# First two tiles of the first down-projection side by side, and three first tiles that meet their last inputs late

## The chip, the cores and the metric

The kernel runs on one core of a Trainium2 chip. The metric is device time of one launch in microseconds (us), as the median of three runs; lower is better. Five engines work side by side and meet only through semaphores: TensorE (PE, with its weight loads as PEld), VectorE (DVE), ScalarE (ACT), GpSimd (POOL) and SyncE (SP), whose queue here does nothing but issue the weight DMAs.

## What is computed

A decoder trunk of two layers over 256 positions and 1024 channels. Layer 0 mixes with a gated MLP and an RWKV-7 recurrence, layer 1 with attention; each layer then has a gated feed-forward part with a causal convolution of width 3. Each half of a layer starts from an RMS norm:

```python
def conv_glu_ffn(h, w_up, conv_w, conv_b, w_down):
    z = h @ w_up
    ...
    z = conv_w[0] * z2 + conv_w[1] * z1 + conv_w[2] * z + conv_b
    gate, val = jnp.split(z, 2, axis=-1)
    return (jax.nn.silu(gate) * val) @ w_down

x = x + conv_glu_ffn(rmsnorm(x, ff_norm[layer]), ...)
```

`w_up` is 1024 x 5632, `w_down` is 2816 x 1024.

## The kernel before

Activations stand with channels on the 128 partitions and the 256 positions along the free axis. The residual `R` has eight such tiles (k = 0 to 7), the hidden layer `H` of a feed-forward part has 22. Every matrix product is made at nearly full fp32 precision from three matmuls per 128 x 128 weight block: operands are split into a high and a low part (`xh`, `xl`; `whi`, `wlo`; `hh`, `hl`), and high x high, high x low and low x high are added in PSUM (`mm3`). A block therefore costs three matmuls of 128 x 256.

**Weights** come in pieces of up to 128 x 1024 in the fixed order of the list `plan`. For each piece SP loads `raw`, ACT makes `whi` (L245) and then DVE makes `wlo` (L246). There are four buffers of each, so the split of a piece waits until PE has finished the piece four places earlier. `piece()` hands pieces out in that order and has two further ones made ahead. DVE and ACT each work through one list of instructions that mixes these splits with the epilogues; so does PE with its matmuls.

**PSUM** gives three buffers `pg` to the large products (`gps()`), each with room for two halves of 256 columns, and five `pm` to others.

**A feed-forward part** (`ffn`) has 22 up-tiles. Tile i is two pieces, the gate half and the value half, eight blocks each, 48 matmuls. Its epilogue goes round four engines: DVE `z` (L963, product times the norm's row `rb`), ACT and DVE the convolution (L967 to L969), ACT silu (L970), POOL gate times value (L971), ACT `hh` (L286), DVE `hl`. In DVE's list `z` of tile i+1 stands behind `hl` of tile i. Then come eight down-tiles d in layer 0: three pieces each, over H tiles 0 to 7, 8 to 14 and 15 to 21 (`DN`), 66 matmuls, one after the other. Each ends in `out_tile`: DVE adds the product to `R`, ACT and DVE make that tile's `xh` and `xl` for the next half of a layer, ACT squares it, POOL adds the square to `sqacc`.

**The first tile of such a half** meets the last of these inputs. Its products can start with k = 0 while tile 7 of `R` is still being made. In the middle of it, after ten of its sixteen blocks, PE sums the squares over the partitions (`norm_stats`, PSUM tile `pst`), DVE and POOL make `rs` from it, and after fifteen blocks PE spreads it into a row (`norm_rows`, `prb`), which DVE copies to `rb`. The epilogue's `z` needs `rb`. In layer 1 the first tile is `values(0)`, whose product goes through `gemm_tm` and needs `rs` alone.

The order on an engine is made by a list scheduler when the program is built, except in the mixers, where PE's order is written out.

Of the kernel before, what the change touches and what calls it, by code (L numbers as in the profile page):

```python
# [12 lines left out]
OP = mybir.AluOpType  # L13
# [4 lines left out]
T = 256  # L18
# [141 lines left out]
def body(nc, tc, A, out):  # L160
# [11 lines left out]
    def mm(o, l, r, start=True, stop=True, shared=False):  # L172
        cnt[0] += 1
        PE.matmul(o, l, r, start=start, stop=stop, skip_group_check=shared)  # L174

    def tt(o, a, b, op, eng=None):
        (eng or V).tensor_tensor(o, a, b, op)  # L177
# [23 lines left out]
    V.tensor_scalar(oka, pc[:, _PC["k_a"]:_PC["k_a"] + 4], -1.0, 1.0, op0=OP.mult, op1=OP.add)  # L201

    DN = ((0, 8), (8, 7), (15, 7))
    AHEAD, LAST = 2, 3
    last = {}

# [8 lines left out]
    def plan_ffn(l):  # L215
        for i in range(2 * FT):
            plan.append((A[f"w_up{l}"][i], KT, 128))
        if l == 1:
            plan.extend((A["w_dn1"][i], 2, 512) for i in range(FT))
            return  # L220
        for d in range(KT):
            for k0, kn in DN:
                plan.append((A[f"w_dn{l}"][d][:, 128 * k0:128 * (k0 + kn)], kn, 128))

    plan_ffn(0)
    plan += [(A["w_qkv"][i], 4, 256) for i in range(8)]
# [120 lines left out]
    def gps():  # L347
        return ps.tile([128, 2, T], F32, name="pg", tag="g", bufs=3)
# [4 lines left out]
    def gemm_fm(o, x):  # L353

        for g in range(2):
            w = piece()
            for k in range(KT):
                mm3(o[:, g], w, k, slice(0, 128), x, k, k == 0, k == KT - 1)
                yield 327

    def gemm_tm(o, x):

        ws = [piece(), piece()]
        for b in range(2):
            sl = slice(128 * b, 128 * b + 128)
            for k in range(KT):
                wh, wl = ws[k // 4][0][:, k % 4], ws[k // 4][1][:, k % 4]
                mm(o[:, b], x[0][:, k, sl], wh, k == 0, False)
                mm(o[:, b], x[0][:, k, sl], wl, False, False)
                mm(o[:, b], x[1][:, k, sl], wh, False, k == KT - 1)  # L370
                yield 327

    def run(g):
        for _ in g:
# [570 lines left out]
    def ffn(l, n, nxt, gname):  # L945
        pool = tc.tile_pool(name=f"ff{l}", bufs=1)
        fp = pool.__enter__()
        H = [fp.tile([128, FT, T], F32R, name=f"h{x}{l}") for x in "hl"]
        if l == 1:
            Rt = fp.tile([128, 2, D], F32, name="Rt")  # L950
            last["pool"] = fp
        for i in range(FT):
            o = gps()
            for y_, _ in enumerate(gemm_fm(o, X)):
                if i == 0 and y_ == 9:
                    norm_stats(n)
                if i == 0 and y_ == 14:
                    norm_rows(n)
            z = fp.tile([128, 2, T + 2], F32, name="z", tag="z", bufs=3)
            if i == 0:  # L960
                fp.tile([128, 248], F32, name="pad_z")
            G.memset(z[:, :, 0:2], 0.0)  # L962
            tt(z[:, :, 2:T + 2], o, n["rb2"], OP.mult)  # L963
            y = fp.tile([128, 2, T], F32, name="y", tag="y", bufs=3)
            for g in range(2):
                ch = i + FT * g
                S.activation(y[:, g], z[:, g, 2:T + 2], AF.Identity, scale=P(f"cw{l}2", ch), bias=P(f"cb{l}", ch))  # L967
                V.scalar_tensor_tensor(y[:, g], z[:, g, 1:T + 1], P(f"cw{l}1", ch), y[:, g], op0=OP.mult, op1=OP.add)  # L968
                V.scalar_tensor_tensor(y[:, g], z[:, g, 0:T], P(f"cw{l}0", ch), y[:, g], op0=OP.mult, op1=OP.add)  # L969
            S.activation(y[:, 0], y[:, 0], AF.Silu)  # L970
            tt(y[:, 0], y[:, 0], y[:, 1], OP.mult, G)  # L971
            split(H[0][:, i], H[1][:, i], y[:, 0])
            if l == 1 and i in (2, 3, 4, 5):
                b, e = i % 2, (i - 2) // 2
                pt = mps()
                for d in range(4):
                    PE.transpose(pt[:, 128 * d:128 * d + 128], R[:, 4 * e + d, 128 * b:128 * b + 128], ident)
                S.copy(Rt[:, b, 512 * e:512 * e + 512], pt)
        if l == 1:
            finish(H, fp, Rt)  # L980
            pool.__exit__(None, None, None)
            return
        for d in range(KT):
            o = gps()
            for k0, kn in DN:
                w = piece()
                for k in range(kn):
                    mm3(o[:, 0], w, k, slice(0, 128), H, k0 + k, k0 + k == 0, k0 + k == FT - 1)
            out_tile(nxt, gname, d, o[:, 0])
        pool.__exit__(None, None, None)  # L990


# [57 lines left out]
    def layer_odd(n, nxt):  # L1050
# [14 lines left out]
        od.tile([128, 16], F32, name="pad_q")  # L1065

        def values(c):
            o = gps()
            for y_, _ in enumerate(gemm_tm(o, X)):
                if c == 0 and y_ == 9:  # L1070
                    norm_stats(n)
                if c == 0 and y_ == 14:
                    norm_rows(n)
            for b in range(2):
                S.activation(vt[:, b, 256 * c:256 * c + 256], o[:, b], AF.Copy, scale=n["rs"][:, b:b + 1])

        def project(j):
            o = gps()
# [118 lines left out]
```

## Time and profile before

| | |
|---|---|
| median of three runs | 685.47 us (684.75 to 685.96) |
| the profiled execution, whole | 685.22 us |
| its span, first to last instruction | 683.4 us |
| PE busy in the span | 646.0 us (95%) |
| DVE busy | 509.3 us (75%) |
| ACT busy | 394.7 us (58%) |
| POOL busy | 108.8 us (16%) |
| mean granted TensorE clock | 0.983 of full |

A busy engine here is one with an instruction in flight; overlapping matmuls count once. The last row says that PE's clock was not full in a few stretches: the profile gives the granted clock, 1.00 or 0.50, of any stretch.

In time the kernel runs: layer 0's mixer to about 174 us, its feed-forward's up-tiles to about 302, its down-tiles to about 372, attention to about 486, the second feed-forward to the end.

### The profile page before, as it was taken

To read this page: it belongs to the slowest core of one execution; us is meant where nothing else is said; L and a number is where in the kernel's file an instruction comes from. 1 tells how busy PE (TensorE), PEld (TensorE's weight loads), DVE (VectorE), ACT (ScalarE), POOL (GpSimd) and SP (SyncE) were. 2 spreads that over 40 slices of the span, in tenths; PEclk is the share of its full clock that TensorE was granted. 3 is DMA by queue.
4 is the path that set the end of the run, shared out by engine and by line. 5 is a ranking of instruction groups with operands and counts; after the bars stand their busy time and mean duration, and the time that the engine had idled before them with its cause. 6 is when DMAs were issued, how large, how long until landed. Compare 5 with 4: busy or idle time off the path is not lost.

```text
span 683.4 us, 14445 instructions
## 1 busy us (share of the span) xinstructions
PE 646.0 (95%) x5766; PEld 611.9 (90%) x5766; DVE 509.3 (75%) x944; ACT 394.7 (58%) x710; POOL 108.8 (16%) x154
## 2 busy tenths in 40 slices
PE   7998988799999999997999999999999999999995
PEld 6897767689899999997999999998899999997895
DVE  6899966747888888886666468885888888888543
ACT  6776433323776666665444457775577666666531
POOL 4100000200422222221112000001222222221000
PEclk9999999989999999998999999999999999999999
DMA  7756264104455555556666563332755555555741
GB/s 250 243 166 210 71 174 102 64 1 152 127 186 186 175 169 181 181 156 171 189 194 205 153 213 123 128 124 66 246 183 181 164 182 186 176 167 188 240 125 62
DMA packets 44915, 110.33 MB, mean 161 GB/s; under 512 B 16432, under 2 KB 18096, under 8 KB 44848
## 3 DMA queue, kind: packets, MB, share of 16 engines
q1 hardware_dynamic: 31104, 105.03, 48.4%
q10 hardware_dynamic: 13584, 3.86, 2.4%
q8 instruction: 45, 0.74, 0.4%
q0 software_dynamic: 160, 0.52, 0.3%
q14 instruction: 22, 0.18, 0.1%
HBM read 106.50 MB, written 2.90 MB: 160 GB/s over the span
## 4 chain that ended last, share of the span: by engine, by line
PE 45%; DVE 29%; POOL 10%; ACT 7%; issue 4%; DMA 3%; ACTq 1%; POOLq 0%; DVEq 0%; SPq 0%
PE pg L174 32%; PE pm L174 11%; DVE wlo L246 10%; POOL y L177 8%; DVE y L968 4%; DVE z L177 4%; ACT y L970 2%; ACT hh L286 2%; DVE y L969 2%; DVE WR L177 2%; ACT whi L245 1%; DVE xl L303 1%; DMA scrA<-BK 1%; DVE ftmp L177 1%; PE pm L1117 1%
## 5 line engine op out<-in xcount | busy, mean ns | idle before, releaser
L174 PE MATMUL pg<-xh,whi 128*128 128x256 f32 x1008 | 286.9, 285 | 0.9 <-ACT whi L245 0.4
L174 PE MATMUL pg<-xh,wlo 128*128 128x256 f32 x1008 | 282.5, 280 | 5.1 <-DVE wlo L246 4.8
L174 PE MATMUL pg<-xl,whi 128*128 128x256 f32 x1008 | 281.4, 279 | 1.2 <-DVE xl L303 1.0
L246 DVE TENSOR_TENSOR wlo<-raw,whi 128x1024 fp32r<-128x1024 f32 (+2 forms) x199 | 234.1, 1182 | 51.9 <-ACT whi L245 51.2
L245 ACT ACTIVATE whi<-raw 128x1024 fp32r<-128x1024 f32 (+2 forms) x199 | 201.1, 1018 | 84.9 <-PE pg L174 55.4
L174 PEld LDWEIGHTS pg<-xh,wlo 128*128 128x128 f32 x1008 | 190.7, 189 | 8.4 <-DVE wlo L246 8.4
L174 PEld LDWEIGHTS pg<-xh,whi 128*128 128x128 f32 x1008 | 190.4, 189 | 6.9 <-issue 3.9
L174 PEld LDWEIGHTS pg<-xl,whi 128*128 128x128 f32 x1008 | 190.6, 189 | 2.7 <-DVE xl L303 1.9
L177 POOL TENSOR_TENSOR y<-y 128x256 f32<-128x256 f32 x44 | 63.5, 1444 | 29.3 <-ACT y L970 28.8
L286 ACT ACTIVATE hh<-y 128x256 fp32r<-128x256 f32 x44 | 18.4, 417 | 71.1 <-POOL y L177 71.1
L174 PE MATMUL pg<-hh,whi 128*128 128x256 f32 x176 | 50.4, 287 | 4.7 <-ACT hh L286 4.7
L177 DVE TENSOR_TENSOR hl<-y,hh 128x256 fp32r<-128x256 f32 x44 | 18.7, 425 | 45.3 <-ACT hh L286 45.3
L967 ACT ACTIVATE y<-z,pc 128x256 f32<-128x256 f32 x88 | 48.1, 594 | 5.9 <-DVE z L177 0.7
L174 PE MATMUL pg<-hh,wlo 128*128 128x256 f32 x176 | 50.4, 287 | 0.0
L174 PE MATMUL pg<-hl,whi 128*128 128x256 f32 x176 | 50.4, 287 | 0.0
L177 POOL TENSOR_TENSOR sqacc<-sqacc,sq 128x256 f32<-128x256 f32 x21 | 18.6, 887 | 169.6 <-ACT sq L311 169.1
L174 PEld LDWEIGHTS pg<-hh,whi 128*128 128x128 f32 x176 | 34.6, 196 | 4.9 <-ACT hh L286 4.9
L969 DVE SCALAR_TENSOR_TENSOR y<-z,pc,y 128x256 f32<-128x256 f32 x88 | 38.5, 479 | 0.0
L968 DVE SCALAR_TENSOR_TENSOR y<-z,pc,y 128x256 f32<-128x256 f32 x88 | 38.5, 479 | 0.0
L174 PEld LDWEIGHTS pg<-hh,wlo 128*128 128x128 f32 x176 | 33.9, 193 | 0.2
L174 PEld LDWEIGHTS pg<-hl,whi 128*128 128x128 f32 x176 | 33.9, 192 | 0.2 <-DVE hl L177 0.2
L962 POOL MEMSET z<- 128x4 f32 x44 | 4.2, 102 | 167.9 <-ACT y L970 151.9
(247 smaller groups left out, 1041.3 us busy)
## 6 DMA issues: line engine op xcount, KB each, us to landing
raw<-w_up SPq DMA_DIRECT2D x88, 512.0 KB, 3.5
raw<-w_dn SPq DMA_DIRECT2D x30, 512.0 KB, 3.6
raw<-w_qkv SPq DMA_DIRECT2D x24, 512.0 KB, 3.5
raw<-w_in SPq DMA_DIRECT2D x20, 512.0 KB, 5.2
raw<-w_dn SPq DMA_DIRECT2D x16, 448.0 KB, 3.4
raw<-ev_wo SPq DMA_DIRECT2D x8, 512.0 KB, 4.0
raw<-od_wo SPq DMA_DIRECT2D x8, 512.0 KB, 4.1
R<-xT SPq DMA_DIRECT2D x4, 256.0 KB, 4.0
```

The lines of the kernel that those rows point to most:

```text
L174: PE.matmul(o, l, r, start=start, stop=stop, skip_group_check=shared)
L177: (eng or V).tensor_tensor(o, a, b, op)
L245: S.activation(hi[:, c], raw[:, c], AF.Copy)
L246: last["lo"] = V.tensor_tensor(lo[:, c], raw[:, c], hi[:, c].bitcast(F32), OP.subtract).ins
L286: S.activation(hi, src, AF.Copy)
L303: V.scalar_tensor_tensor(x[1][:, k], R[:, k], P(gname, k), x[0][:, k].bitcast(F32), op0=OP.mult, op1=OP.subtract)
L962: G.memset(z[:, :, 0:2], 0.0)
L967: S.activation(y[:, g], z[:, g, 2:T + 2], AF.Identity, scale=P(f"cw{l}2", ch), bias=P(f"cb{l}", ch))
L968: V.scalar_tensor_tensor(y[:, g], z[:, g, 1:T + 1], P(f"cw{l}1", ch), y[:, g], op0=OP.mult, op1=OP.add)
L969: V.scalar_tensor_tensor(y[:, g], z[:, g, 0:T], P(f"cw{l}0", ch), y[:, g], op0=OP.mult, op1=OP.add)
L970: S.activation(y[:, 0], y[:, 0], AF.Silu)
L1117: PE.transpose(pt[:, 128 * i:128 * i + 128], sc[:, 128 * i:128 * i + 128], ident)
```

## The change

Three edits with one idea, and nothing of the arithmetic changes but the order of additions between tiles.

1. The first two down-tiles of layer 0 are made side by side: `DOWN` lists their pieces in the order (0, first), (1, first), (0, second), (1, second), (0, third), (1, third), and then d = 2 to 7 as before. The loads, splits and products all follow that list, and two `pg` buffers are held at once.
2. `gemm_first`, for the first up-tile of both feed-forward parts: gate and value half get a `pg` buffer each, and the blocks go k = 0 to 4 of the gate half, 0 to 4 of the value half, then 5 to 7 of each. The `z` of this tile becomes two instructions of 256 columns.
3. `gemm_tm` does the same for `values(0)`, with the two blocks of positions in place of the halves.

```diff
+    DOWN = [(d, *part) for part in DN for d in range(2)] + [(d, *part) for d in range(2, KT) for part in DN]
...
+    def gemm_first(o, x):
+
+        ws = [piece(), piece()]
+        for ks in (range(0, 5), range(5, KT)):
+            for g in range(2):
+                for k in ks:
+                    mm3(o[g], ws[g], k, slice(0, 128), x, k, k == 0, k == KT - 1)
+                    yield 327
...
+        late = isinstance(o, list)
+        for ks in ((range(0, 5), range(5, KT)) if late else (range(KT),)):
+            for b in range(2):
+                sl, ob = slice(128 * b, 128 * b + 128), o[b] if late else o[:, b]
+                for k in ks:
...
-            o = gps()
-            for y_, _ in enumerate(gemm_fm(o, X)):
+            o = [gps()[:, 0], gps()[:, 0]] if i == 0 else gps()
+            for y_, _ in enumerate(gemm_first(o, X) if i == 0 else gemm_fm(o, X)):
...
-            tt(z[:, :, 2:T + 2], o, n["rb2"], OP.mult)
+            if i == 0:
+                for g in range(2):
+                    tt(z[:, g, 2:T + 2], o[g], n["rb"], OP.mult)
+            else:
+                tt(z[:, :, 2:T + 2], o, n["rb2"], OP.mult)
...
-        for d in range(KT):
-            o = gps()
-            for k0, kn in DN:
-                w = piece()
-                for k in range(kn):
-                    mm3(o[:, 0], w, k, slice(0, 128), H, k0 + k, k0 + k == 0, k0 + k == FT - 1)
-            out_tile(nxt, gname, d, o[:, 0])
+        os = {}
+        for d, k0, kn in DOWN:
+            if k0 == 0:
+                os[d] = gps()[:, 0]
+            w = piece()
+            for k in range(kn):
+                mm3(os[d], w, k, slice(0, 128), H, k0 + k, k0 + k == 0, k0 + k == FT - 1)
+            if k0 + kn == FT:
+                out_tile(nxt, gname, d, os.pop(d))
```

What it makes of the engines' lists, at three places. First PE, where the first piece of down-tile 0 ends; before (`pg_3924` is down-tile 0, `whi_3881` its second piece):

```order
L174 MATMUL pg_3924<-hh0_2259,whi_3851 128x256
L174 MATMUL pg_3924<-hl0_2260,whi_3851 128x256
L174 MATMUL pg_3924<-hh0_2259,wlo_3852 128x256
L174 MATMUL pg_3924<-hh0_2259,whi_3881 128x256
L174 MATMUL pg_3924<-hl0_2260,whi_3881 128x256
```

and now (`pg_3957` is down-tile 1, `whi_3883` its first piece):

```order
L174 MATMUL pg_3926<-hh0_2259,whi_3853 128x256
L174 MATMUL pg_3926<-hl0_2260,whi_3853 128x256
L174 MATMUL pg_3926<-hh0_2259,wlo_3854 128x256
L174 MATMUL pg_3957<-hh0_2259,whi_3883 128x256
L174 MATMUL pg_3957<-hl0_2260,whi_3883 128x256
```

Where tile 0 went on to its second piece, tile 1 now has its first; on ACT, DVE and SP the pieces are exchanged in the same way, and nothing else of their lists moves there.

Second DVE, at the first up-tile of layer 0's feed-forward; before (`wlo_2352` and `wlo_2382` are the pieces of up-tile 2, which take the buffers of up-tile 0's two pieces; `rs` to `z` is the norm and the tile's `z`):

```order
L246 TENSOR_TENSOR wlo_2264<-raw_2262,whi_2263 128x1024
L303 SCALAR_TENSOR_TENSOR xl_86<-R_73,pc_74,xh_85 128x256 x2
L246 TENSOR_TENSOR wlo_2294<-raw_2292,whi_2293 128x1024
L333 TENSOR_SCALAR rs_2307<-pst_2304 128x1 x2
L246 TENSOR_TENSOR wlo_2352<-raw_2350,whi_2351 128x1024
L343 COPY rb_2329<-prb_2326 128x256
L177 TENSOR_TENSOR z_2334<-pg_2261,rb_2329 128x2x256
L246 TENSOR_TENSOR wlo_2382<-raw_2380,whi_2381 128x1024
L968 SCALAR_TENSOR_TENSOR y_2338<-z_2334,pc_74,y_2338 128x256 x2
```

and now (`wlo_2354` and `wlo_2384` are those of up-tile 2):

```order
L247 TENSOR_TENSOR wlo_2265<-raw_2263,whi_2264 128x1024
L304 SCALAR_TENSOR_TENSOR xl_86<-R_73,pc_74,xh_85 128x256 x2
L334 TENSOR_SCALAR rs_2308<-pst_2305 128x1 x2
L247 TENSOR_TENSOR wlo_2271<-raw_2269,whi_2270 128x1024
L247 TENSOR_TENSOR wlo_2354<-raw_2352,whi_2353 128x1024
L344 COPY rb_2330<-prb_2327 128x256
L247 TENSOR_TENSOR wlo_2384<-raw_2382,whi_2383 128x1024
L177 TENSOR_TENSOR z_2335<-pg_2261,rb_2330 128x256
L177 TENSOR_TENSOR z_2335<-pg_2262,rb_2330 128x256
L984 SCALAR_TENSOR_TENSOR y_2340<-z_2335,pc_74,y_2340 128x256
```

The second split of up-tile 2 stood behind `z` and now stands ahead of it, and `rs` moved ahead of one split. In the second feed-forward that split is moved past `z` too.

Third PE in `values(0)`, ahead of `pst`; before (`whi_4591` and `whi_4618` are the tile's two pieces, k = 0 to 3 and 4 to 7):

```order
L174 MATMUL pg_4670<-whi_4618,xl_86 128x256
L174 MATMUL pg_4670<-whi_4591,xh_85 128x256
L174 MATMUL pg_4670<-wlo_4592,xh_85 128x256
L174 MATMUL pg_4670<-whi_4591,xl_86 128x256
...
L174 MATMUL pst_4713<-cst_79,sqacc_2255 128x1 x2
```

and now:

```order
L174 MATMUL pg_4673<-whi_4620,xh_85 128x256
L174 MATMUL pg_4673<-wlo_4621,xh_85 128x256
L174 MATMUL pg_4673<-whi_4620,xl_86 128x256
L174 MATMUL pst_4716<-cst_79,sqacc_2255 128x1 x2
L174 MATMUL pg_4672<-whi_4620,xh_85 128x256
```

Before, all eight blocks of the first half stood ahead of `pst`, k = 7 among them; now k = 0 to 4 of both halves stand there, and k = 5 to 7 (`pg_4672`) come behind it. `pst` keeps its place after 30 matmuls.

## Rows read from the trace of the kernel before

**Rows 1.** Waits of PE, whole kernel: waiter, awaited, us in total, times, longest.

```profile
PE pg L174 <- ACT hh L286: 4.7, 1, 4.7
PE pg L174 <- DVE xl L303: 1.5, 4, 0.5
...
PE pst L174 <- POOL sqacc L177: 0.8, 1, 0.8
```

**Rows 2.** Stretches at the first down-tile: busy us (count) by engine, granted clock, DMA.

```profile
312.50:315.09 2.59, 0.00 (x0) 0.00 (x0) 1.53 (x4) 0.88 (x3) 1.39 (x1) 0.50 0.67 176
315.09:319.33 4.24, 4.24 (x18) 4.07 (x19) 3.45 (x5) 2.55 (x4) 0.00 (x0) 0.50 0.61 177
```

**Rows 3.** Timeline of PE, down-tiles 0 and 1: start, us, instruction, [idle before].

```profile
305.35 0.28 PE L174 MATMUL pg<-hh,whi 128*128 128x256 f32 x1
...
310.12 0.28 PE L174 MATMUL pg<-hh,wlo 128*128 128x256 f32 x1
315.09 0.58 PE L174 MATMUL pg<-hh,whi 128*128 128x256 f32 x1 [4.70 <-ACT hh L286]
...
319.34 0.29 PE L174 MATMUL pg<-hh,whi 128*128 128x256 f32 x1
...
325.36 0.28 PE L174 MATMUL pg<-hh,whi 128*128 128x256 f32 x1
```

**Rows 4.** Waits of DVE over 20 up-tiles, 196 to 310 us.

```profile
DVE hl L177 <- ACT hh L286: 21.6, 20, 1.1
```

**Rows 5.** Timeline of DVE and ACT, last up-tiles and down-tile 0.

```profile
304.51 1.08 DVE L246 TENSOR_TENSOR wlo<-raw,whi 128x896 fp32r<-128x896 f32 x1
...
310.20 1.23 DVE L246 TENSOR_TENSOR wlo<-raw,whi 128x1024 fp32r<-128x1024 f32 x1
...
312.93 1.08 DVE L246 TENSOR_TENSOR wlo<-raw,whi 128x896 fp32r<-128x896 f32 x1
...
315.91 1.09 DVE L246 TENSOR_TENSOR wlo<-raw,whi 128x896 fp32r<-128x896 f32 x1 [0.41 <-ACT whi L245]
...
314.62 0.42 ACT L286 ACTIVATE hh<-y 128x256 fp32r<-128x256 f32 x1 [1.56 <-POOL y L177]
```

**Rows 6.** Timeline of PE, POOL and ACT, first up-tile of layer 0.

```profile
174.20 0.28 PE L174 MATMUL pg<-xh,whi 128*128 128x256 f32 x1
...
181.19 0.50 PE L174 MATMUL pst<-cst,sqacc 128*128 128x1 f32 x4
...
183.71 0.71 PE L174 MATMUL prb<-cst,rs 128*128 128x128 f32 x4
...
177.87 1.96 POOL L177 TENSOR_TENSOR sqacc<-sqacc,sq 128x256 f32<-128x256 f32 x2 [0.59 <-ACT sq L311]
182.04 1.62 POOL L334 TENSOR_TENSOR rs<-rs,cst 128x2 f32<-128x2 f32 x1 [2.21 <-DVE rs L333]
...
184.70 1.06 ACT L245 ACTIVATE whi<-raw 128x1024 fp32r<-128x1024 f32 x1 [3.06 <-PE pg L174]
...
186.79 1.06 ACT L245 ACTIVATE whi<-raw 128x1024 fp32r<-128x1024 f32 x1
```

**Rows 7.** Timeline of PE, POOL and ACT, first up-tile of layer 1.

```profile
490.87 0.60 PE L174 MATMUL pst<-cst,sqacc 128*128 128x1 f32 x4 [0.79 <-POOL sqacc L177]
...
491.81 0.71 POOL L334 TENSOR_TENSOR rs<-rs,cst 128x2 f32<-128x2 f32 x1 [1.00 <-DVE rs L333]
...
495.01 1.06 ACT L245 ACTIVATE whi<-raw 128x1024 fp32r<-128x1024 f32 x1 [2.22 <-PE pg L174]
...
497.78 1.06 ACT L245 ACTIVATE whi<-raw 128x1024 fp32r<-128x1024 f32 x1 [0.66 <-ACT y L967]
```

**Rows 8.** Timeline of PE, `values(0)`.

```profile
374.59 0.28 PE L174 MATMUL pg<-wlo,xh 128*128 128x256 f32 x1
375.37 0.39 PE L174 MATMUL pg<-whi,xl 128*128 128x256 f32 x1 [0.50 <-DVE xl L303]
```

**Rows 9.** Stretches in layer 0's mixer, columns as in rows 2.

```profile
57.55:59.66 2.11, 0.01 (x1) 0.04 (x1) 2.01 (x5) 2.09 (x7) 0.00 (x0) 1.00 0.93 322
59.92:63.33 3.41, 3.41 (x36) 3.07 (x32) 3.38 (x7) 0.58 (x2) 0.00 (x0) 0.50 0.85 246
```

More of the change, by code (lines that the diff above doesn't have):

```diff
@@ L220, in plan_ffn @@
             return
-        for d in range(KT):
-            for k0, kn in DN:
-                plan.append((A[f"w_dn{l}"][d][:, 128 * k0:128 * (k0 + kn)], kn, 128))
+        for d, k0, kn in DOWN:
+            plan.append((A[f"w_dn{l}"][d][:, 128 * k0:128 * (k0 + kn)], kn, 128))
     plan_ffn(0)
@@ L359, in gemm_fm @@
                 yield 327
+    def gemm_first(o, x):
[5 more added lines that the diff above has]
+                    yield 327
     def gemm_tm(o, x):
         ws = [piece(), piece()]
[L364 to L371, printed above, removed]
+        late = isinstance(o, list)
[3 more added lines that the diff above has]
+                for k in ks:
+                    wh, wl = ws[k // 4][0][:, k % 4], ws[k // 4][1][:, k % 4]
+                    mm(ob, x[0][:, k, sl], wh, k == 0, False)
+                    mm(ob, x[0][:, k, sl], wl, False, False)
+                    mm(ob, x[1][:, k, sl], wh, False, k == KT - 1)
+                    yield 327
     def run(g):
@@ L982, in ffn @@
             return
-        for d in range(KT):
-            o = gps()
-            for k0, kn in DN:
-                w = piece()
-                for k in range(kn):
-                    mm3(o[:, 0], w, k, slice(0, 128), H, k0 + k, k0 + k == 0, k0 + k == FT - 1)
-            out_tile(nxt, gname, d, o[:, 0])
+        os = {}
+        for d, k0, kn in DOWN:
+            if k0 == 0:
[5 more added lines that the diff above has]
+                out_tile(nxt, gname, d, os.pop(d))
         pool.__exit__(None, None, None)
@@ L1067, in values @@
         def values(c):
-            o = gps()
+            o = [gps()[:, 0], gps()[:, 0]] if c == 0 else gps()
             for y_, _ in enumerate(gemm_tm(o, X)):
@@ L1074, in values @@
             for b in range(2):
-                S.activation(vt[:, b, 256 * c:256 * c + 256], o[:, b], AF.Copy, scale=n["rs"][:, b:b + 1])
+                S.activation(vt[:, b, 256 * c:256 * c + 256], o[b] if c == 0 else o[:, b], AF.Copy, scale=n["rs"][:, b:b + 1])
         def project(j):
```

## The prediction

> **What bounds the kernel now.** I read the page first: PE is busy 95% of the span, so a gain can only come from stretches in which PE waits, or runs below its full clock. Next the list of PE's waits. The longest by far is one wait of 4.7 us for `hh`, and the inputs of the three first tiles add 1.5 us for `xl` in four waits and 0.8 us for the sum of squares [rows 1]. The granted clock says the rest: it is 0.50, that is 1.2 GHz, from 312.50 to 319.33, which begins inside the wait for `hh` and lasts 4.2 us beyond it [rows 2]. Last I looked at who is late in the feed-forward itself. Over 20 up-tiles DVE waits 21.6 us, 1.1 us in each, for `hh` of the tile before, with the next tile's product long done [rows 4]. So the up-tiles are paced by the epilogue's round over DVE, ACT and POOL, and PE has slack there. That decides what each edit is worth: at the down-tiles and in attention PE's time is the kernel's time; at a first up-tile only what reaches the epilogue counts.
>
> **Down-tiles 0 and 1.** Between 319.34 and 325.36 there are 51 steps, 0.118 us each at full clock [rows 3]. *What is lost now:* the step from 310.12 to 315.09 took 4.97 in place of 0.118, so 4.85 us; the 18 steps from 315.09 to 319.34 took 4.25 in place of 2.12, so 2.13 us, partly the half clock, partly the 0.4 us until `hl` [rows 2, 3]. Together 7.0 us.
>
> *What comes in its place.* H tile 21 is needed after 63 matmuls now, and after 24+24+21+21+18 = 108 with the change. The second piece of tile 0 starts at 305.35, so its first did 24 steps earlier, at 302.52 [rows 3]. 108 steps of 0.118 lead to 315.27, plus what PE loses on the way to the weights, which arrive just in time here. Nothing in DVE's list moves but the sizes of pieces, so the splits end near the times of the splits that stand there now: 1024 columns cost 1.23 where 896 cost 1.08 [rows 5]. The first now ends at 304.51 + 1.23, about 305.8, against a need at 305.59 (third matmul of a piece): 0.2 late. The fourth piece's ends near 311.4 (the 310.20 row, 0.14 later and 0.15 shorter) against 311.2: 0.2 late. The fifth's at 314.05 against 314.0, with the 0.14 shift. Each late split costs also one slow step of 0.22, seen in every such place. So PE wants H tile 21 at about 316.1, and `hh` is there at 315.04, `hl` 0.5 later [rows 5]: the wait is covered with 1 us to spare. The sixth piece's split stands behind that `hl` and ends at 317.0, as now [rows 5]; PE wants it at 316.7 and loses about 0.5. Sum of the new stalls: 0.3+0.3+0.3+0.5 = 1.4 us. PE then starts tile 2 at 302.52 + 132 x 0.118 + 1.4 = 319.5. Before, it did at 325.36 [rows 3]. **Gain 5.9 us.** The most is 7.3 (no stall at all); the least that I can construct is 3.0, if at each of four boundaries a whole split of 1.2 us more were missing. I take 5.9, since each split has its row. The extra `pg` buffer costs nothing: it was freed by a `z` that ended before 305. No idle of more than 0.5 us remains; the fall here, and one in the mixer [rows 9], followed about 2 us of it, so nothing should lower the clock.
>
> **`values(0)`.** PE steps from 374.59 to 375.37, 0.66 us more than 0.118, for `xl` of the last tile [rows 8]. With the change that block comes after 30 others and `pst`, about 1.8 us later, when it is there. The squares were ready for `pst` at its old time without a wait, and 0.7 us earlier they still are, by 0.5 us. PE is the bound around it: **gain 0.66 us**, bounds 0.4 and 0.7.
>
> **First up-tile of layer 0.** PE loses some 2 us there now, but what counts is when `z` of this tile and its epilogue run. From 174.20 the new order has 34 matmuls ahead of `pst`, so PE is there at 178.4; the squares are complete at 177.87 + 1.96 = 179.83 [rows 6]. PE idles 1.5 us there: the waits for `xl` are gathered into this one. `pst` at 179.87 in place of 181.19, and the same 2.5 us from `pst` to `prb` as now (181.19 to 183.71), puts `prb` at 182.4; PE has only 11 matmuls between and idles 0.8 us again. Three matmuls later the tile's product is done, at 183.4, a good 1 us earlier than now. But DVE's list now has the split of up-tile 2's second piece ahead of `z`. This split needs the buffer that the tile's own last matmuls read: ACT's half runs now at 184.70, ended by PE [rows 6]; it will at 183.4, ends at 184.5, DVE's takes until 185.7. Only then `z`, in two halves; the convolution follows its first half at 186.15, and ACT's next split, which is behind it, starts at 187.2 where it now starts at 186.79 [rows 6]. From there the lists are the same. **Loss 0.4 us.** The uncertain term is POOL's power for `rs`: 1.62 beside a DVE split [rows 6], 0.71 without one [rows 7]. With 0.71 everything is 0.8 us earlier, a gain of 0.4. I take 1.62, since a split again stands right behind `rs` on DVE.
>
> That `z` cannot pass the split is what rows 4 show 20 times: `z` of the next tile stands behind `hl`, and waits with it. The Trainium skill says the same as a rule (PSUM — Partial Sum Buffer, Engine vs sequencer instructions: ScalarE and VectorE queues are strict FIFO), and it speaks against this edit: by it the tile loses 0.4 us; could `z` pass, it would run at 183.8 and the edit would gain about 1.5. The trace agrees with the rule.
>
> **First up-tile of layer 1.** `pst` waits for the squares and starts at 490.87 now [rows 7]; the new order only exchanges what PE does ahead of it, so it starts at 490.87 again, after one idle of 1.4 us. Behind it stand 18 matmuls of the tile in place of 26, so the product is done about 0.9 us earlier. Again the split goes ahead of `z`: ACT's half at 494.1 in place of 495.01 [rows 7], done 495.15, DVE's done 496.5, `z` first half 496.86, the convolution to 497.95, and ACT's next split there, now at 497.78 with 0.66 of waiting ahead of it [rows 7]. **Loss 0.15 us**, bounds: a loss of 0.9 (what the convolution's start is late by), a gain of 0.9 (what PE is early by).
>
> **Sum.** 5.9 + 0.66 - 0.4 - 0.15 = 6.0 us. The profiled execution took 685.22 in all, 0.25 below the median of 685.47, so the changed kernel should take 679.2 in such an execution and a median of **679.4 us**. A third of the gain at the down-tiles is the clock, the rest the cover; the edits at the first up-tiles bring nothing.
>
> **Rivals.** *The first up-tiles pay.* If POOL's power takes 0.71 and the splits wait less than I say, PE's lead of 0.9 us at each tile arrives: 679.4 - 0.55 - 0.9 to 1.8, so 677.0 to 678.0. For it: PE loses those waits now. Against it: rows 4 and the moved split. 13%.
>
> *The clock falls at a first up-tile.* The change gathers scattered waits into 1.5 and 0.8 us of idle within 4 us in layer 0, and 1.4 us in layer 1. The trace has a fall after 2.1 us of idle, and half clock for 3.4 us then [rows 9], 6.8 at the down-tile [rows 2]. Half pace costs 45% of such a stretch, 1.5 or 3.0 us, of which 0.75 is slack before the second tile's `z` is held up: 0.8 to 2.3 us for each tile it happens to, so 680.2 to 684.0. Against it: both first tiles have 1 to 1.5 us of scattered idle now and keep full clock. The Trainium skill (TensorE: Matmul & The Clock Gate, A second HAM failure mode: psum-queue depth-cycling) says that frequent micro-idles between groups of matmuls make the clock oscillate; by it this rival would be the rule, and the first tiles would already fall now, which the trace doesn't show. 14%.
>
> *The side-by-side pieces starve PE,* so that the wait moves from `hh` to `wlo`: the 3.0 bound, 682.3. The splits' rows speak against it. 7%.
>
> *The round of the up-tiles gets longer.* The same 21.6 us of waiting [rows 4] say that any delay in the round is paid once per tile, 40 times in both parts. If PE's new lead over the round pushed an ACT split ahead of `hh` and this cost 0.15 us a tile, the whole gain would be gone; from (6.0 + 1.4)/40 = 0.19 us it is slower, and 0.25 would give 689.4. Against it: the engines' lists in the round are row for row the same. 4%.
>
> **Chances.** The forecast, 678.6 to 680.4 with the small terms' bounds: 62%. The range 677.8 to 681.8 holds it, most of the first rival and over half of the second. About 0.2%, 1.4 us, is what a measurement can tell from no change; faster by more 93%, within 3%, slower 4%.
>
> **What would show it.** In the changed profile: no wait of 4.7 us for `hh` and full clock over the whole down-projection; short waits for `wlo` at piece ends, and tile 2 some 17 us after tile 0 (22.8 now); no wait for `xl` in `values(0)`; at the first up-tiles one wait for `sqacc` of about 1.5 us, a `z` in two halves behind a split, and up-tiles at the same pace of 6 us. Wrong would be a half clock near those tiles, a wait over 1 us for `wlo` between the down-tiles, or a longer round.

## The result, and the profile after

The changed kernel takes **676.49 us** (676.43 to 676.56) against 685.72 (684.75 to 687.24): a ratio of 0.9871 with an interval of 0.984 to 0.9902, so 9.2 us or 1.3% faster. The forecast was 679.4, the range 677.8 to 681.8: the sign was right, and the gain half as large again as foretold. The profiled execution of after took 676.43 us, with a span of 674.7 against 683.4, so 8.8 us lie in the two traces. I cut both spans at the same instructions. "Last R" is the last addition to `R` ahead of a first tile, "hl 21" the last `hl` of a feed-forward part, "tile 2" and "tile 7" the additions of those down-tiles to `R`. The third column is the measured difference (negative is a gain), the fourth the prediction's.

| stretch, us | before | after | difference | forecast |
|---|---|---|---|---|
| start to last R of layer 0 | 176.61 | 176.25 | -0.36 | 0 |
| last R to hl 21, layer 0 (first up-tile) | 138.46 | 139.66 | +1.20 | +0.4 |
| hl 21 to tile 2 | 18.26 | 11.94 | -6.32 | -5.9 |
| tile 2 to tile 7 | 38.87 | 37.40 | -1.47 | 0 |
| tile 7 to the end of the values | 24.65 | 23.74 | -0.91 | -0.66 |
| to last R of layer 1 | 91.84 | 91.70 | -0.14 | 0 |
| last R to hl 21, layer 1 (first up-tile) | 137.80 | 137.62 | -0.18 | +0.15 |
| hl 21 to the end | 56.93 | 56.33 | -0.60 | 0 |

What was foretold is easy to find. First PE's waits in the kernel after (columns as in [rows 1]), three of the groups:

```profile
PE pg L174 <- DVE wlo L247: 3.6, 6, 1.4
...
PE pst L174 <- POOL sqacc L177: 2.0, 2, 1.3
...
PE prb L174 <- POOL rs L335: 1.5, 2, 0.8
```

The 4.7 us for `hh` of [rows 1] are gone, and so are the four waits for `xl`. In their place stand the waits for the squares and for `rs` at the first up-tile of layer 0, near the forecast of 1.5 and 0.8 us (1.30 and 0.64, below). In layer 1 PE waits 0.68 us for the squares (up to 1.2 in later profiles of that order), where 1.4 was worked out and before had 0.79. Next the two waits of PE over 0.2 us in the timeline of the down-tiles 0 and 1, after:

```profile
312.31 0.39 PE L174 MATMUL pg<-hh,wlo 128*128 128x256 f32 x1 [0.30 <-DVE wlo L247]
...
317.90 0.39 PE L174 MATMUL pg<-hh,wlo 128*128 128x256 f32 x1 [0.27 <-DVE wlo L247]
```

Only weights are waited for, and the clock is full throughout, where [rows 2] had 6.8 us at half. The cover is there as worked out: `hh` of H tile 21 ends at 315.88, and PE comes to it 1.0 us later.

```profile
315.46 0.42 ACT L287 ACTIVATE hh<-y 128x256 fp32r<-128x256 f32 x1 [1.57 <-POOL y L177]
```

```profile
316.89 0.28 PE L174 MATMUL pg<-hh,whi 128*128 128x256 f32 x1
```

Then the first up-tile of layer 0: PE's timeline, and below it stretches with columns as in [rows 2], whose last three are the granted clock, the DMA share and GB/s.

```profile
179.51 0.60 PE L174 MATMUL pst<-cst,sqacc 128*128 128x1 f32 x4 [1.30 <-POOL sqacc L177]
182.14 1.05 PE L174 MATMUL prb<-cst,rs 128*128 128x128 f32 x4 [0.64 <-POOL rs L335]
...
182.35:185.77 3.42, 3.42 (x18) 3.42 (x18) 2.16 (x3) 1.06 (x1) 0.00 (x0) 0.50 0.81 235
185.77:189.20 3.43, 3.43 (x31) 3.43 (x31) 2.95 (x8) 2.73 (x4) 0.10 (x1) 1.00 0.64 209
```

The two waits came as worked out, and behind them the granted clock is 0.50, that is 1.2 GHz, for 3.4 us, with 18 matmuls where the next stretch has 31. The rival that the clock falls at a first up-tile (14%) happened in this execution.

What nobody had foretold is the fourth line of the table. These are DVE's additions of the down-tiles 2 to 4 to `R`, in the timeline of before and then of after:

```profile
333.33 0.42 DVE L177 TENSOR_TENSOR R<-R,pg 128x256 f32<-128x256 f32 x1 [0.46 <-PE pg L174]
341.10 0.42 DVE L177 TENSOR_TENSOR R<-R,pg 128x256 f32<-128x256 f32 x1 [0.47 <-PE pg L174]
348.88 0.42 DVE L177 TENSOR_TENSOR R<-R,pg 128x256 f32<-128x256 f32 x1 [0.46 <-PE pg L174]
```

```profile
327.86 0.42 DVE L177 TENSOR_TENSOR R<-R,pg 128x256 f32<-128x256 f32 x1 [0.36 <-PE pg L174]
335.34 0.42 DVE L177 TENSOR_TENSOR R<-R,pg 128x256 f32<-128x256 f32 x1 [0.37 <-PE pg L174]
342.82 0.42 DVE L177 TENSOR_TENSOR R<-R,pg 128x256 f32<-128x256 f32 x1 [0.37 <-PE pg L174]
```

A tile takes 7.77 us before and 7.48 after. It is the same 66 matmuls, in the same order, without a wait of PE, at a granted clock of 1.00 in both. Per matmul that is 117.8 against 113.3 ns from start to start. The change doesn't touch these tiles. In tile 2 the same difference of 0.29 us stands in the third line of the table. What makes the step, and whether it belongs to the change, is the main question of the experiments.

### The profile page after: what moved, and what is told of

Read it like the earlier page. It is cut to its first block, busy times and chain, and to the rows that moved or that the text cites. A ratio compares the mean times of both kernels' runs of the same rounds, so it can differ in the third digit from the quotient of the medians.

```text
span 674.7 us, 14452 instructions
## 1 busy us (share of the span) xinstructions
PE 644.9 (96%) x5766; PEld 615.4 (91%) x5766; DVE 509.2 (75%) x946; ACT 394.5 (58%) x710; POOL 108.8 (16%) x154
## 4 chain that ended last, share of the span: by engine, by line
PE 65%; DVE 20%; POOL 5%; ACT 4%; issue 3%; DMA 3%; SPq 0%; POOLq 0%; ACTq 0%; DVEq 0%
PE pg L174 50%; PE pm L174 14%; DVE wlo L247 6%; POOL y L177 3%; DVE WR L177 2%; DVE y L984 2%; DVE z L177 2%; ACT y L986 1%; DVE y L985 1%; ACT hh L287 1%; DMA scrA<-BK 1%; DVE ftmp L177 1%; PE pm L1135 1%; DVE xl L304 1%; DMA R<-xT 1%
## 5 line engine op out<-in xcount | busy, mean ns | idle before, releaser
L174 PE MATMUL pg<-xh,whi 128*128 128x256 f32 x1008 | 290.0, 288 | 0.6 <-ACT whi L246 0.6
L174 PE MATMUL pg<-xl,whi 128*128 128x256 f32 x1008 | 284.3, 282 | 0.1
L174 PEld LDWEIGHTS pg<-xh,whi 128*128 128x128 f32 x1008 | 192.5, 191 | 6.3 <-issue 3.9
L174 PEld LDWEIGHTS pg<-xl,whi 128*128 128x128 f32 x1008 | 192.7, 191 | 0.8 <-DVE xl L300 0.3
L174 PE MATMUL pg<-hh,whi 128*128 128x256 f32 x176 | 48.7, 277 | 0.0
L174 PE MATMUL pg<-hl,whi 128*128 128x256 f32 x176 | 48.7, 277 | 0.0
L174 PEld LDWEIGHTS pg<-hh,whi 128*128 128x128 f32 x176 | 33.1, 188 | 0.0
```

## The experiments

### One edit at a time

Theory A: the step is settled anew each time PE's even flow is broken, and no property of the order of pieces. Theory B: the new order brings the shorter step. The four kernels also price each edit by itself.

The kernel before with edit 1 alone:

```diff
+    DOWN = [(d, *part) for part in DN for d in range(2)] + [(d, *part) for d in range(2, KT) for part in DN]
...
+        for d, k0, kn in DOWN:
```

> The kernel before with edit 1 alone (the first two down-tiles side by side). What is settled by the two traces: tile 2 starts 6.3 us earlier. In question is the further 1.5 us that down-tiles 3 to 7 gained, since their matmuls step by 113.3 ns instead of 117.8. Theory A: which of the two steps holds is settled anew each time PE restarts after a wait, and is no property of the order of the pieces; then the gain is 6.3 us, with 1.5 to 2.2 us on top or not by chance, so 679.4 or 677.6 us, and the up-tiles, values and second down-projection show either step too, without a system. Theory B: the new order itself brings the shorter step; then down-tiles 3 to 7 step by 113.3 ns again, as in the changed kernel, and the time is 677.6 to 677.9.

The changed kernel without edit 2:

```diff
-            o = [gps()[:, 0], gps()[:, 0]] if i == 0 else gps()
-            for y_, _ in enumerate(gemm_first(o, X) if i == 0 else gemm_fm(o, X)):
+            o = gps()
+            for y_, _ in enumerate(gemm_fm(o, X)):
```

> The changed kernel without its edit 2: the first up-tiles of both feed-forward parts as in the kernel before. Theory: edit 2 is a loss, 1.2 us in layer 0 (of which the half clock after the wait for the squares is most) and 0.15 in layer 1, so this kernel takes 676.5 - 1.35 = 675.1 us and its first up-tile shows full clock throughout. Rival: what was lost at the first up-tile of layer 0 comes from the mixer ending as it does, not from the edit; then 676.3 to 676.6 with half clock again. With the longer step of the matmuls in the down-tiles, 1.5 to 2.2 us more in either case.

The kernel before with edit 2 in layer 0 alone, and in layer 1 alone:

```diff
+            first = i == 0 and l == 0
-            for y_, _ in enumerate(gemm_fm(o, X)):
+            for y_, _ in enumerate(gemm_first(o, X) if first else gemm_fm(o, X)):
```

```diff
+            first = i == 0 and l == 1
-            for y_, _ in enumerate(gemm_fm(o, X)):
+            for y_, _ in enumerate(gemm_first(o, X) if first else gemm_fm(o, X)):
```

> The kernel before with edit 2 in layer 0 alone. Theory: half clock after the two waits of the tile for sqacc and rs, hl of up-tile 21 some 1.2 us later than before; after it everything as before, so 685.7 + 1.2 = 686.9 us, within 1.5 us since the matmuls' step may fall either way downstream. Rival, the forecast of the prediction: no fall, a loss of 0.4 us. If order brings the shorter step (theory B of the first run), the down-tiles of this kernel step by 117.8 ns; if chance (theory A), either.

> The kernel before with edit 2 in layer 1 alone. Theory: full clock at that tile, hl of its up-tile 21 within 0.2 us of before as measured from the sum of squares; 685.7 us within 0.3, or up to 1.5 less where the down-tiles fall into the shorter step of 113.3 ns (theory A of the first run; by theory B they do not).

Measured, beside 685.38 us (683.17 to 690.42) for before on the same chip:

| kernel | median (lowest to highest), us | ratio and interval | layer 0: last R to hl 21 | hl 21 to tile 2 | tiles 2 to 7 | tile 7 to end of values | layer 1: last R to hl 21 | after the last matmul |
|---|---|---|---|---|---|---|---|---|
| edit 1 | 679.3 (678.32 to 684.13) | 0.9922 [0.9891, 0.9953] | 138.65 | 12.31 | 38.87 | 24.65 | 138.24 | 7.36 |
| edits 1, 3 | 678.67 (676.34 to 679.81) | 0.9896 [0.9871, 0.9922] | 138.62 | 11.95 | 37.40 | 23.74 | 139.32, clock fell | 6.76 |
| edit 2, layer 0 | 685.77 (684.02 to 688.72) | 1.0004 [0.9989, 1.0019] | 138.78 | 17.63 | 37.40 | 24.65 | 139.78, clock fell | 7.36 |
| edit 2, layer 1 | 683.9 (681.62 to 688.35) | 0.9976 [0.9948, 1.0004] | 138.48 | 17.72 | 37.40 | 24.66 | 137.63 | 7.35 |

Theory B falls. With the old order of pieces tiles 2 to 7 took 37.40 us in both kernels with edit 2, with the new order 38.87 in the one with edit 1. The matmuls' records of one tile show it too; first edit 1 alone, then edit 2 in layer 0 (groups by line and shape: count, busy us, mean ns of one):

```profile
L174 PE MATMUL pg<-hh,wlo 128*128 128x256 f32 x21 | 5.9, 281 | 0.0
```

```profile
L174 PE MATMUL pg<-hh,wlo 128*128 128x256 f32 x22 | 6.1, 276 | 0.0
```

A record is 281 ns long where the step is 117.8, 276 where it is 113.3. Edit 1 alone gives 6.1 us, near what the prediction forecast for it. At an equal step it is worth 17.63 or 17.72 less 11.95, so **5.7 us**, against the 5.9 of the sum; the repeat of before (below), also at the short step, has 18.18, which makes it 6.2, since half clock there lasts 1 us further past hl 21. Edit 3 shows as 24.65 to 23.74 in all kernels, **0.9 us**, and the tail behind the last matmul is 7.35 to 7.36 in all kernels without edit 3 and 6.75 to 6.77 in all with it, another **0.6** that I can't explain. ACT issues the last output 0.28 us sooner there (0.84 after the start of its last `zg` in after, 1.12 in before):

```profile
678.45 0.51 ACT L1046 ACTIVATE zg<-zg,rs 128x256 f32<-128x256 f32 x1 [1.11 <-POOL rs L320]
679.57 0.34 ACTq L1047 DMA_DIRECT2D out<-zg  x1
```

```profile
670.29 0.51 ACT L1064 ACTIVATE zg<-zg,rs 128x256 f32<-128x256 f32 x1 [1.11 <-POOL rs L321]
671.13 0.34 ACTq L1065 DMA_DIRECT2D out<-zg  x1
```

Edit 2 in layer 0 didn't make the clock fall here; the loss is 0.13 to 0.32 us against the old orders of this chip and before. Without edit 2 in layer 1 the clock fell there in two of three kernels. The kernel without edit 2 was expected at 675.1 us and took 678.67. Its stage in layer 0 is 1.0 us shorter than in the profile of after, as expected, but the fall in layer 1 cost 1.7; and its profiled execution, at 676.34, was the shortest of its six, so the stages do not explain its median.

### The same programs once more, and two ways to mend the first up-tile

The changed kernel, unaltered:

> The changed kernel once more, unaltered. Theory A (the matmuls' step of 113.3 or 117.8 ns is settled at each restart after a wait, by chance; so is whether the clock falls near a first up-tile): its stages show other steps than in the first profile, at least one of down-tiles 3 to 7, the up-tiles of layer 0 or the second down-projection, and its runs scatter by 1 to 4 us around 677 to 679. Rival: the steps belong to the program; then the same steps stand in the same stages, 117.8 to 306 us, 113.3 from 318 to 366, and the runs repeat 676.5.

The changed kernel with `z` ahead of the split that stood in front of it:

```diff
-        last["lo"] = V.tensor_tensor(lo[:, c], raw[:, c], hi[:, c].bitcast(F32), OP.subtract).ins
+        with tc.issue_after(last["z"]) if len(made) == last.get("held") else nullcontext():
+            last["lo"] = V.tensor_tensor(lo[:, c], raw[:, c], hi[:, c].bitcast(F32), OP.subtract).ins
...
+                last["held"] = used[0] + 3
```

> The changed kernel with z of both first up-tiles ahead of the split of up-tile 2's second piece on DVE. By the prediction's account the split ahead of z is what eats PE's lead, and z ahead of it gains about 1.5 us in layer 0 and 0.9 in layer 1, so 2.4 us less than the changed kernel on the same chip. Theory now: the round of the up-tiles starts from z of up-tile 1, which PE's product releases; z of up-tile 0 has slack, and moving it gains nothing: z of up-tile 0 comes 1.2 us earlier, z of up-tile 1 within 0.2 us of where it was, and the time stays within 0.5 us.

The changed kernel with one more small matmul at the start of each of five down-tiles:

```diff
+            if k0 == 0 and d > 2:
+                N = (0, 0, 0, 16, 32, 64, 128, 192)[d]
+                pd = mps()
+                mm(pd[:, 0:N], w[0][:, 0, 0:128], H[0][:, 0, 0:N])
```

> The changed kernel with one more matmul at the start of each of the down-tiles 3 to 7, of 16, 32, 64, 128 and 192 columns into a PSUM tile that nobody reads. Its own cost is at most 0.4 us in all. It breaks the even flow of the matmuls without a wait. Theory A1: any break settles the step anew, so the five tiles show 113.3 in some and 117.8 ns in others. Theory A2: only a wait for another engine does; then all five tiles have one step, whichever.

The changed kernel with the norm's steps later on PE:

```diff
-                if i == 0 and y_ == 9:
+                if i == 0 and y_ == 13:
                     norm_stats(n)
-                if i == 0 and y_ == 14:
+                if i == 1 and y_ == 5:
                     norm_rows(n)
+                    tail(0, o0)
```

> The changed kernel with the norm's steps moved back on PE: the sum of squares after 14 of the tile's 16 blocks in place of 10, the spreading into a row after 6 blocks of up-tile 1 and, with it, the epilogue of up-tile 0. If the round starts from PE's product of up-tile 1, the idle of 1.3 and 0.64 us for sqacc and rs is what edit 2 pays, and without it up-tile 1's product comes 2 us earlier after the last R than in the kernel before, hl of up-tile 21 of layer 0 1.5 to 2.6 us earlier than before (137.0 to 135.9 us after the last addition to R in place of 138.5), in layer 1 0.7 to 1.5 us; in all 2 to 4 us less than the changed kernel, 673 to 675 us. Rival: the round starts from hl of up-tile 0, that is from the norm; then z of up-tile 1 is early but hl of up-tile 1 is not, and the time is that of the changed kernel within 0.5 us.

On this chip before took 685.77 us (684.77 to 689.17).

| kernel | median (lowest to highest), us | ratio and interval | layer 0: last R to hl 21 | tiles 2 to 7 | layer 1: last R to hl 21 | hl 21 to the end |
|---|---|---|---|---|---|---|
| changed kernel | 676.48 (675.99 to 676.99) | 0.9857 [0.983, 0.9883] | 138.84 | 37.40 | 137.65 | 56.33 |
| `z` first | 677.23 (675.89 to 678.01) | 0.9866 [0.984, 0.9892] | 138.93, clock fell | 37.40 | 137.26 | 57.00 |
| extra matmuls | 676.86 (676.04 to 677.77) | 0.9862 [0.9835, 0.989] | 138.88 | 39.15 | 137.67 | 55.17 |
| norm later | 676.2 (675.27 to 676.31) | 0.9849 [0.9823, 0.9876] | 138.71 | 37.40 | 138.08 | 56.34 |

*The changed kernel again.* The clock did not fall this time, after the same two waits in the same program:

```profile
180.18 0.61 PE L174 MATMUL pst<-cst,sqacc 128*128 128x1 f32 x4 [1.30 <-POOL sqacc L177]
182.81 0.71 PE L174 MATMUL prb<-cst,rs 128*128 128x128 f32 x4 [0.62 <-POOL rs L335]
...
183.02:186.44 3.42, 3.42 (x31) 3.42 (x31) 2.57 (x5) 1.07 (x1) 0.00 (x0) 1.00 0.75 228
```

So the tile costs 138.84 - 138.46 = **0.4 us** at full clock, the forecast, and 0.8 more where the clock falls. The step in the up-tiles of layer 0 was 113.3 ns, 117.8 in the first profile. It was 113.3 again in tiles 2 to 7, so the repeat speaks for theory A only in part.

*`z` first.* In layer 1 `z` comes 6.54 us after last R instead of 7.56 in the repeat, 1.0 us earlier, and of that 0.39 us is left at hl 21 (137.26 against 137.65). The `hl` of up-tiles 0 and 1 are still 0.65 us earlier (13.27 against 13.92 for the first); the rest goes in up-tiles 4 and 5, which take 0.12 us more each in this execution, as in four other profiles, both orders among them; why is open. In layer 0 the clock fell, and hl 21 is 0.7 us earlier than in the changed kernel's fall. So the split ahead of `z` costs something, as the prediction said, but 0.4 to 0.65 of the 1.0 us. My later theory, nothing at all, is wrong too. The median shows none of it.

*Norm later.* In layer 0 PE's waits for the squares and for `rs` are gone:

```profile
180.75 0.50 PE L174 MATMUL pst<-cst,sqacc 128*128 128x1 f32 x4
184.01 0.61 PE L174 MATMUL prb<-cst,rs 128*128 128x128 f32 x4
```

and `z` of up-tile 1 is 0.7 us earlier (12.56 after last R, 13.27 in the repeat). But hl 21 is only 0.13 us earlier in layer 0 and 0.4 later in layer 1. PE's idle there is not what the round waits for: the rival held, and the idle counts only through the clock.

*Extra matmuls.* Tile 2 stepped by 113.3 ns, then the five tiles by 117.8, 117.8, 113.3, 117.8, 117.8; the additions to `R` of tiles 4 to 6 show one short tile, 7.62 us, and one long, 7.89:

```profile
342.44 0.42 DVE L177 TENSOR_TENSOR R<-R,pg 128x256 f32<-128x256 f32 x1 [0.46 <-PE pg L174]
350.06 0.42 DVE L177 TENSOR_TENSOR R<-R,pg 128x256 f32<-128x256 f32 x1 [0.36 <-PE pg L174]
357.95 0.42 DVE L177 TENSOR_TENSOR R<-R,pg 128x256 f32<-128x256 f32 x1 [0.46 <-PE pg L174]
```

None of the five extra matmuls waits for another engine. So a break without any wait can change the step, and within a tile it holds: theory A1.

### What sets the step, and how much cover edit 1 needs

The changed kernel with an extra matmul of 64 columns at eleven places, and the same with 512:

```diff
+                mm(mps()[:, 0:64], H[0][:, 0, 0:128], H[0][:, 0, 0:64])
```

```diff
+                mm(mps()[:, 0:512], H[0][:, 0, 0:128], H[0][:, 0:2])
```

> The changed kernel with one more matmul of 64 columns, whose result nobody reads, at eleven places: the starts of down-tiles 3 to 7, of values 1 to 3, and at three pieces of the second half of the second down-projection. In the run with extra matmuls of five widths the matmuls after the one of 64 columns stepped by 113.3 ns, after the other four by 117.8. Theory W: the width of the break sets the step; then all eleven stretches here step by 113.3, which saves 0.30 us a tile where it was 117.8 (values, second down-projection, 2 us in all) and costs 0.06 x 11 = 0.7 us, so 675 us. Theory C: chance at each break; then both steps among the eleven stretches.

> The same with 512 columns in place of 64. A longer matmul gives the weight loads behind it time to catch up, as a wait for weights does, after which 113.3 ns was the more frequent step (215 of 299 stretches in ten traces). Theory W: all eleven stretches at 113.3 ns, whatever the one of 64 does. Theory C: both steps. The extra columns cost some 0.23 x 11 = 2.5 us, so 679 us.

The kernel before, unaltered:

> The kernel before once more, unaltered. Its down-tiles 3 to 7 stepped by 117.8 ns in the profile on which the prediction rests, by 113.3 in the two kernels that had only an edit 2. Theory A (chance): down-tiles 3 to 7 may show 113.3 ns here, and then are 37.4 us long in place of 38.87; its up-tiles and second down-projection may also differ from the first profile. Rival: the step belongs to the program, so 117.8 again, with 38.87.

The changed kernel with tile 1's second piece behind tile 0's last:

```diff
+    DOWN = [(0, *DN[0]), (1, *DN[0]), (0, *DN[1]), (0, *DN[2]), (1, *DN[1]), (1, *DN[2])] + [(d, *part) for d in range(2, KT) for part in DN]
```

> The changed kernel with the down-tiles 0 and 1 only half side by side: both first pieces, then the rest of tile 0, then the rest of tile 1. PE comes to H tile 21 after 24 + 24 + 21 + 18 = 87 matmuls in place of 108. By the prediction's account, in which the cover of 108 matmuls is 1 us more than needed, 87 leave a wait of 2.5 - 1.0 = 1.5 us for hh, so tile 2 comes 1.0 to 1.5 us later after hl of up-tile 21 than with the change (11.95), 13.0 to 13.5 us, and if the clock falls after the wait up to 15. Rival: the splits and not hh set PE's pace there; then within 0.4 us of 11.95.

*The widths.* With 64 columns (678.65 us, 677.12 to 679.28, where theory W has 675) tiles 3 to 7 stepped by 113.3, the values mostly and the second down-projection throughout by 117.8: nearly each stretch kept the step that it had. With 512 (678.85, one run) it was 113.3 in tiles 3 to 7, and both in the values and at the end. The width doesn't set the step; theory W falls.

*Before again.* 687.91 us (one run), tiles 2 to 7 in 37.40 us, where the first profile had 38.87. One program, both steps: theory A holds, and the 1.5 us of the table's fourth line don't need the change. How often each program takes which step these profiles don't show: before has one of each, the changed kernel the short one twice. In this execution the clock fell at the first up-tile of layer 0 with the **old** order:

```profile
180.55:183.96 3.41, 3.41 (x16) 3.13 (x16) 1.77 (x2) 1.06 (x1) 0.36 (x1) 0.50 0.58 178
183.96:187.38 3.42, 3.42 (x18) 3.42 (x17) 1.36 (x3) 0.00 (x0) 1.63 (x1) 0.50 0.56 190
187.38:190.80 3.42, 3.42 (x31) 3.42 (x31) 2.67 (x5) 2.60 (x4) 0.00 (x0) 1.00 0.21 87
```

It lasted 6.8 us and cost 141.04 - 138.46 = 2.6 us, or 2.4 against the old order's 138.62 to 138.65 in the kernels that also have the long step there.

*Half the cover.* PE waits for `hh` once more, for the 1.5 us that the count of matmuls gives:

```profile
316.54 0.38 PE L174 MATMUL pg<-hh,whi 128*128 128x256 f32 x1 [1.53 <-ACT hh L287]
```

Tile 2 comes 13.27 us after hl 21 (forecast 13.0 to 13.5), 1.3 more than with the change, and the clock stayed full. The median is 678.48 (677.3 to 679.81). So the cover of edit 1 is as the prediction reckoned it.

### The order inside a triple, and the best of the stages

> The changed kernel with edit 2 left out in layer 0 and, in layer 1, with z ahead of the split of up-tile 2's second piece. From the stages measured so far, counted from the last addition to R to hl of up-tile 21: layer 0 138.5 to 138.6 (old order at full clock) in place of 138.8 to 139.7, layer 1 137.26 (z first) in place of 137.65. So 0.7 us less than the changed kernel where its clock held, 1.4 where it fell: 675.8 or 675.1 us. Rival: the old order in layer 0 falls as often (one of five profiles, to 141.0); then no difference that can be measured.

```diff
+            first = i == 0 and l == 1
+            o = [gps()[:, 0], gps()[:, 0]] if first else gps()
```

> The changed kernel with another order inside each triple, so that no stationary block is loaded twice in a row: high x high, low weight x high, high weight x low for the feature-major products, and in the same way for values and the second down-projection. Theory D: loading the same block twice in a row is what makes the step of 117.8 ns possible; then all stretches step by 113.3, values and the second down-projection save 1.0 and 1.2 us, and the time is 674.3 us or a little less, unless the earlier need of the low weights (0.12 us in each wait for them) takes some of it back. Theory C: it is chance at each break whatever the order; then both steps appear again, and the time is 676 to 678.

The edit of the feature-major products; those of values and of the second down-projection are turned in the same way:

```diff
         mm(o, wh, xh, start, False)
-        mm(o, wh, xl, False, False)
-        mm(o, wl, xh, False, stop)
+        mm(o, wl, xh, False, False)
+        mm(o, wh, xl, False, stop)
```

Beside 685.2 us (683.14 to 689.06) for before: with the other order 687.19 (682.75 to 689.51), ratio 1.0027 [1.0003, 1.0051]. Tiles 3 to 7 stepped by 117.8 ns, the up-tiles of layer 0 by 113.3, so loading one block twice in a row is not the cause; theory D falls. Both theories missed the time. Seven of the ten us lost lie in layer 0's mixer, 184.0 us where the changed kernel has 176 to 177: PE waits 7.1 us for `bw` of DVE there and 2.6 us for a DMA, waits that no other trace shows at such length. The mixed kernel took 676.43 (675.25 to 680.04), ratio 0.9877 [0.9848, 0.9906], with the foretold stages, 138.65 and 137.26, but not the foretold 675.1 to 675.8. No version that I ran beats the changed kernel by more than the runs scatter.

## Why the prediction missed

*Down-tiles 0 and 1: right.* 5.7 to 6.2 us at an equal step, 6.3 between the two profiles, 5.9 forecast. Counted as the sum counts, from the start of tile 0 to that of tile 2, it is 22.84 before and 16.84 after, 6.0 us. The four late splits cost 0.3, 0.6, 0.2 and 0.5 us with their slow steps, 1.6 where the sum has 1.4, and the shorter step in part of the stretch made up for it. The clock stayed full, and half the cover gave back what the count of matmuls says. The bound of 3.0 doesn't follow from its words, four whole splits of 1.2 us, which would leave about 1; nothing came near it.

*First up-tile of layer 0: right at full clock, the rival in the profile.* ACT's split behind the convolution starts 10.59 us after last R in the repeat, exactly as worked out, and the loss of 0.4 us was met to 0.02. The second agreement is in part luck: over all full-clock profiles the old order took 138.46 to 138.65 (five) and the new one 138.78 to 138.91 (four), a loss of 0.1 to 0.45. But the clock fell in five of the nine profiles with that order and the wait of 1.3 to 1.4 us, and where `z` stood behind the split that cost 0.7 to 0.9 us more. So 14% was too little for that rival, and its price was at the low end of 0.8 to 2.3. The old order is not safe either: it fell in one of six profiles, for 2.6 us. That the same waits were there without a fall in one trace, which the prediction used against the rival, proves little.

*First up-tile of layer 1: the path right, its length mis-sized.* A loss of 0.15 was forecast. As foretold, `z` came later than before (7.56 us after last R, 6.61 before), and the 0.66 us that ACT's next split had waited took up the delay. But this split starts 9.01 us after last R, where the sum let the convolution end at 9.26; before it was 9.09. These are DVE's `z` and that split after, last R being at 480.70:

```profile
488.26 0.75 DVE L177 TENSOR_TENSOR z<-pg,rb 128x256 f32<-128x256 f32 x2
```

```profile
489.71 1.05 ACT L246 ACTIVATE whi<-raw 128x1024 fp32r<-128x1024 f32 x1
```

So 0.08 us is won there instead of 0.17 lost, and 0.14 at the first `hl`. With `z` behind the split, hl 21 came 137.62 to 137.73 us after last R in all eight profiles, and no clock fell. With the old order it took 137.80, 138.24 and 138.26 at full clock, and 139.32 and 139.78 where it fell. The prediction's 137.80 was the best of these five. In the two at 138.2 PE's longer step held ACT's split until 9.19, so there PE's lead counted, and up-tiles 4 and 5 were 0.12 us longer each. So edit 2 gains 0.1 to 0.6 here at full clock.

*`values(0)`: mis-sized.* 0.66 forecast, 0.91 measured, and the same in every pair of kernels. All of it is there by `pst`, 4.11 us after tile 7's addition before, 3.20 after. The sum had only the wait in [rows 8]. It left out the slow step behind the wait (0.227 us in place of 0.118), which it did count at the down-tiles, and the shorter step of the other 30 matmuls gave 0.13. Where before has the short step (edit 2 in layer 0), the wait itself is that much longer.

*What the sum did not have: the step that failed.* It took 117.8 ns as the price of a matmul at full clock, from one stretch of [rows 3], and put every stage that the edits don't touch at nothing. The price was one of two, and the other stood in the same trace, in the up-tiles. That is 1.5 us in the tiles 2 to 7 of these two profiles and 0.3 in tile 2, with no need of the change. The tail's 0.6 us came with edit 3. The mixer's 0.36, the same code, varied: it ended at 175.5 to 179.4 us over the runs that leave it alone.

So of the 2.8 us of span that the sum was short, 1.8 is the step's and 0.4 the mixer's; 0.6 is the tail, 0.3 each edit 3 and layer 1, 0.1 each edit 1 and the rest of attention, and layer 0's fallen clock took 0.8 back. The range, 1.6 us below and 2.4 above, held only the uncertainty of the edits: neither the step nor the tail had a term in it.

That accounts for the two profiles. It doesn't account for all of the median: 9.2 us on the first chip and 9.3 on the second, whose intervals begin at 6.7 and 8.0. Single runs of before scatter over 7 us on another chip (683.17 to 690.42), but its medians on five chips lie between 685.14 and 685.77, so one unlucky execution is no explanation. At an equal step and full clock the stages give edit 1 5.7 to 6.2, edit 3 0.9 and the tail 0.6, layer 1 0.1 to 0.6 and layer 0 a loss of 0.1 to 0.45, together 7 to 8. Whether the other one to two us are noise, or the changed kernel takes the short step more often, stays open.

## What to carry to other kernels

Cover for a late operand can be counted in matmuls ahead of its first use, and the count held to 0.2 us here with all of the cover and with half of it. Before a price from one stretch goes into a sum, look whether the same instruction costs the same elsewhere in the trace, and whether the code that isn't changed takes the same time in a second profile. Small differences between two profiles belong to the change only when each stage is compared at the same matmul step and the same granted clock.

## What the runs showed of the hardware that I had not expected

The same 128x256 matmul has **two steady steps at a granted clock of 1.00**, 113.3 and 117.8 ns. It keeps one over up to hundreds of matmuls, and changes it where the flow is broken, by a wait or by another matmul in between; without a break it changed only where the values' products pass into the projections', in five of sixteen traces. Behind waits that make a step of 215 to 235 ns, some 320 of 440 stretches of 20 or more matmuls ran at 113.3 in fifteen traces and the rest at 117.8. In the long step of the down-tiles one weight load of three is 192 ns long instead of 188, always that of the same place in the triple, here the first, over 30 us of before (groups of weight loads: count, busy us, mean ns):

```profile
L174 PEld LDWEIGHTS pg<-hh,whi 128*128 128x128 f32 x86 | 16.5, 192 | 0.0
L174 PEld LDWEIGHTS pg<-hl,whi 128*128 128x128 f32 x86 | 16.1, 188 | 0.0
L174 PEld LDWEIGHTS pg<-hh,wlo 128*128 128x128 f32 x85 | 16.0, 188 | 0.0
```

In the kernel with edit 1 alone it was the second. None of the three, the order of the pieces, the width of the break and the order in the triple, settles the step; what does stays open.

Whether the clock falls after a wait of 1.3 us is not settled by the program either. The Trainium skill (TensorE: Matmul & The Clock Gate, A second HAM failure mode: psum-queue depth-cycling) says of a bf16 kernel of 512 columns that its frequent micro-idles between groups of matmuls made the clock oscillate. The traces agree in part: the old order's scattered waits were followed by a fall in one of six profiles in layer 0 and two of five in layer 1. The gathered waits were followed by one in five of nine in layer 0 (1.3 to 1.4 us, and up to 0.7 behind it) and in none of ten in layer 1 (0.7 to 1.2 us).
